# First mixer of a two-layer encoder step: attention chunks read back into the place of their own low parts, and the last value projection in two passes

## The chip, the cores and the metric

The kernel runs on one core of a Trainium2 chip. It is one inference step of a two-layer encoder trunk, all in 32-bit floating point at its inputs and outputs. The metric is the device time of one execution in microseconds (us). Engines: TensorE (PE, with its weight loads PEld), VectorE (DVE), ScalarE (ACT), GpSimd (POOL) and SyncE (SP). SP does no arithmetic here; it issues most of the loads, in order. GpSimd issues the stores and a few loads.

## The reference

1024 prompt rows and 128 sample rows (8 streams of 16), 1152 in all, each 1024 wide, go through two layers. Only the first layer's mixer is touched by the change:

```python
def stick_breaking(q, k, v, q_pos, k_pos):
    z = jnp.einsum('bqhd,bkhd->bhqk', q, k).astype(jnp.float32) * (HEAD_DIM ** -0.5)
    mask = k_pos[None, :] < q_pos[:, None]
    log_keep = jnp.where(mask, jax.nn.log_sigmoid(-z), 0.0)
    between = lax.cumsum(log_keep, axis=3, reverse=True) - log_keep
    w = jnp.where(mask, jnp.exp(jax.nn.log_sigmoid(z) + between), 0.0)
    return jnp.einsum('bhqk,bkhd->bqhd', w.astype(v.dtype), v)

q, k, v, u = ab_project(h, w_in)                # 8 heads of 64, and a gated convolution input u
a_out = stick_breaking(q, k, v, ...)            # 512 columns
c_out = silu(layernorm(depthwise_conv31(u)))    # 512 columns
out = jnp.concatenate([a_out, c_out], axis=-1) @ w_out
```

The layer's input is normalised (RMS) ahead of the projection, the mixer's output is added to the input, and a squared-ReLU MLP follows. The second layer has banded softmax attention in place of the two branches.

## The kernel before, in words

**Data layout.** Activations lie transposed: 128 of the 1024 columns are one *chunk*, with all 1152 rows along the free dimension, cut into three *groups* of 384 (G, NG). Every operand of a dense product is split into a high and a low part (`split`, L183: ScalarE copies the high part, VectorE subtracts it), and each product is three matmuls (`SPLIT`: high·high, high·low, low·high). The eight chunks of a mixer's input, high and low, lie in sixteen fixed tiles, `a{c}{i}` with chunk c and part i (`place`, L231). The eight chunks of the mixer's output, called `cat0`, are put in the same sixteen places later: 0 to 3 are the four pairs of attention heads, 4 to 7 the convolution.

**Steps.** Work is written as lists of `Step`s (L45): a piece of code with its planned TensorE time (`pe`, in ns), a planned VectorE time (`dve`), and, where needed, a name, the name of a step that it comes after, and a lag in planned time behind that step. `merge` (L53) interleaves several lists so that each advances at the same share of its own total; a step whose predecessor or lag isn't due lets the others go first. `level` spreads convolution taps among the result by VectorE time. The framework then writes one instruction queue per engine, in about that order, but takes an instruction ahead when by its own estimates its data and its buffers are ready. On the chip each queue runs in order, and an instruction that waits holds up all behind it.

**Dense products.** `chunk_steps` (L310) makes one output chunk: a step that loads weights ahead, and for each of the three groups two halves of 12 matmuls (`dense`, L215, `per=12`: input chunks 0 to 3, then 4 to 7) into one PSUM bank, and an eviction. There are eight PSUM banks, all of one pool (`bank`, L143).

**First mixer** (`mixer0`, L657). The heads go in four pairs, p = 0 to 3. Stage p does pair p's attention; merged with it are the projection of pair p+1 (`proj`, L872: queries, keys, values, into tiles `sq`, `sk`, `sv`), the cached attention of the sample streams (`sample_steps`, L546), and convolution taps on VectorE. `expand_qk` (L887) makes the attention operands of a pair from `sq` and `sk` (VectorE at L351 and L353). `expand_v` (L906) turns the values: VectorE differences (L903), transposes on TensorE (L913), copies on ScalarE (L915). An attention job has two score steps (L943 to L947, then scans on VectorE, L923 to L929) and a tail (transposes L388, products L398, and the end of a piece in L411 and L412). Each pair's finished pieces go to DRAM (`cat_d`, L363) for p < 3; pair 3's are split directly into chunk 3 of `cat0`.

**Stage 3** has no projection to fill it. In its place it does the first part of the output projection, `part_out` (L1088): input chunks 0 to 2 of `cat0` for all eight output chunks, in passes of 6 and 3 matmuls, added to the input (`xo`, in the places of `sq` and `sv`, loaded by `old`, L1094), and stored. `first` is the weight load and the first passes of 6 of output chunk 0, which need input chunks 0 and 1 only. Beside it runs `conv_norm` (L1020), the layer norm of the convolution output, which reads it from DRAM and writes chunks 4 to 7. The rest of the output projection (chunks 3 to 7) follows in `rest` (L1299).

**What the change touches.** Chunks 0 to 2 come back from DRAM in `ready_chunks` (L1075): for each chunk one load of 1152 columns into the tile `sk` (one buffer, before that pair 3's keys), and three splits from it into the chunk's two places. In stage 3's list of fill work stand, in this order, chunks 0 and 1, `first`, chunk 2 (3000 ns of planned time after the last step carried over from pair 2), and 5000 ns behind it the rest of `part_out`.

Of the kernel before, what the change touches and what calls it, by code (L numbers as in the profile page):

```python
# [9 lines left out]
F32R = mybir.dt.float32r  # L10
# [114 lines left out]
def tile_trunk(ctx, tc, ins, outs):  # L125
# [17 lines left out]
    def bank(name):  # L143
        return psum.tile([P, 512], F32, tag="ps", name=name)
# [109 lines left out]
    def new_hs(name):  # L254
        return [[new_h(g, half, name) for half in range(2)] for g in range(NG)]
# [54 lines left out]
    def chunk_steps(n, got, ahead, h, ks, evac, name, depth=1, per=12):  # L310

        steps = [Step(0.0, lambda: [ahead(n + d) for d in range(depth + 1)], 1200.0)]
        for g in range(NG):
            box = {}

            def ps(g=g, box=box):
                if "p" not in box:
                    box["p"] = bank(f"ps{name}{g}")
                return box["p"]

            steps += dense(ps, lambda: got[n], h, g, ks, per)
            steps.append(Step(0.0, lambda g=g, ps=ps: evac(ps(), g), 470.0))
        return steps

    def chunks_steps(ns, got, ahead, h, ks, evac, name, depth=1):

# [330 lines left out]
    def mixer0():  # L657
        with ExitStack() as st:
# [213 lines left out]
            def proj(p):  # L872
                steps = []
                for n, tag in enumerate(("sq", "sk", "sv")):
                    def evac(ps, g, n=n, tag=tag):
                        if g == 0:
                            S[tag, p] = pp.tile([P, T], F32, tag, f"{tag}0{p}")
                        if g < 2:
                            tt(S[tag, p][:, g * G:g * G + G], ps[:, :G], rstd[g], ALU.mult)
                        else:  # L880
                            ACT(S[tag, p][:, g * G:], ps[:, :G], AF.Copy)
                        if g == 2 and n:
                            put(outs["sb_k" if n == 1 else "sb_v"][p], S[tag, p])
                    steps += chunk_steps(at[4 * n + p], got, ahead, h, ks, evac, f"p{p}{n}")
                return steps

# [98 lines left out]
            for p in range(4):  # L985
                S["p"] = p
                expand_qk(p)
                if p < 3:
                    fill = proj(p + 1)
                    if p < 2:  # L990
                        fill[10:10] = ag(p + 2)
                    n = TAPS[p + 1]
                    mix, now, taps = [], taps[:n], taps[n:]
                else:
                    cat_t = new_hs("cat0")
                    (first, fill), now = part_out(0, range(3), pp, cat_t), []
                    for s in taps:
                        s.pe = 900.0
                    mix = taps + conv_norm(lambda: (conv_pool.close(), Bufs(st.enter_context(pool("ln")), t1=3, yl=5))[1],
                                           cat_t)  # L1000
                cat = Cat(0, p, wk, cat_t)
                jobs = attend(p, cat)
                body, left = pipeline(jobs[1:], jobs[0][2])
                steps = carry + [jobs[0][0]] + [Step(327.0, lambda p=p, g=g: expand_v(p, g)) for g in range(NG)]
                if p == 3:
                    late, = ready_chunks(0, [2], pp, cat_t)
                    late.name, late.after, late.lag = "ready", carry[-1].name, 3000.0
                    fill[0].after, fill[0].lag = "ready", 5000.0
                    fill = ready_chunks(0, range(2), pp, cat_t) + first + [late] + fill
                steps += [jobs[0][1]] + body  # L1010
                carry = left
                if p == 3:
                    steps += carry
                cs = sample_out(cat, wk, p)
                load = sample_caches(0, p, cp)
                sample = two_samples(*(sample_steps(0, p, bg, S, wk, load, soft, cs) for bg in range(2)))
                run(level(merge(steps, sample, fill, mix), now))
            return cat_t

    def conv_norm(new_pool, cat_t):  # L1020

        steps = []

        pools = []

        def norm(g):
            box = {}

            def load():
                if g == 0:  # L1030
                    pools.append(new_pool())
                box["y"] = [pools[0].tile([P, G], F32, "yl", f"yl{g}{c}") for c in range(4)]
                for c in range(4):
                    put(box["y"][c], cat_d[0][4 + c, :, g * G:g * G + G])

            def centre():
                yl = box["y"]
                mu = bank(f"mu{g}")
                for c in range(4):
                    mm(mu[:, :G], ones, yl[c], start=c == 0, stop=c == 3)  # L1040
                for c in range(4):
                    stt(yl[c], mu[:, :G], -1.0 / 512, yl[c], ALU.mult, ALU.add)

            def squares():
                yl, box["acc"] = box["y"], None
                for c in range(4):
                    box["acc"] = add_square(box["acc"], yl[c], pools[0], f"l{g}{c}")

            def scale():
                box["r"] = pools[0].tile([P, G], F32, "r", f"rl{g}")  # L1050
                diag, box["rows"], _ = rstd_of(box["r"], pools[0], box["acc"], 1.0 / 512, LN_EPS, f"l{g}")
                diag(box["acc"])

            def out(c):
                y = box["y"][c]
                tt(y, y, box["r"], ALU.mult)
                s = pools[0].tile([P, G], F32, "t1", f"ls{g}{c}")
                gg, bb = cvec[:, 1, c:c + 1], cvec[:, 2, c:c + 1]
                ACT(s, y, AF.Sigmoid, bias=bb, scale=gg)
                ACT(y, y, AF.Identity, bias=bb, scale=gg)  # L1060
                tt(y, y, s, ALU.mult)
                split(cat_t[g][1][0][:, c, :], cat_t[g][1][1][:, c, :], y)

            name = f"ln{g}"
            return ([Step(50.0, load, 0.0, f"l{name}"),
                     Step(2600.0, centre, 1900.0, f"c{name}", f"l{name}", 4000), Step(500.0, squares, 1400.0),
                     Step(700.0, scale, 1200.0, f"s{name}", f"c{name}", 5000),
                     Step(800.0, lambda: box["rows"](), 0.0, None, f"s{name}", 2500)]
                    + [Step(300.0, lambda c=c: out(c), 1500.0) for c in range(4)])

        for g in range(NG):
            steps += norm(g)
        return steps

    def ready_chunks(layer, chunks, pp, cat_t):  # L1075

        steps = []
        for c in chunks:
# [5 lines left out]
                    split(hi, lo, cr[:, g * G:g * G + G])  # L1084
            steps.append(Step(300.0, go))
        return steps

    def part_out(layer, ks, pp, cat_t):  # L1088

# [900 lines left out]
```

## Time and profile before

Times of three runs: 2721.12, 2721.54 and 2724.41 us; the median is 2721.54.

| | |
|---|---|
| profiled execution | 2724.12 us |
| its span, first to last instruction | 2722.3 us |
| mean granted TensorE clock | 0.993 |
| TensorE / weight loads | 2667.6 / 2555.7 us busy |
| VectorE / ScalarE / GpSimd | 2038.3 / 1362.9 / 330.2 us busy |
| DMA | 422.89 MB, mean 155 GB/s |

A row of a view in stretches gives the stretch and its length, then each engine's busy time in it with the count of instructions, the granted clock as a share of full speed, the busy share of the 16 DMA engines and GB/s. A row of a timeline gives start, duration, engine, line of the kernel, operation, output and inputs by the program's names, shapes and count; in brackets stands the idle time of the engine ahead of it and what ended it. A row of a list of waits gives who waited for whom: us in total, times, longest. A row of the chain of waits gives start, duration and what the time went to. TensorE records overlap (the next starts inside the one before), so the cost of a pass is read from start to start.

### The profile page before, as it was taken

The numbers are of one execution on the slowest core, as the hardware profiler recorded it, in microseconds if no ns is written. First come the engines' busy times: TensorE is split into PE (matmuls) and PEld (weight loads), VectorE is DVE, ScalarE is ACT, GpSimd is POOL, SyncE is SP. The second block draws the span as 40 slices with busy tenths as digits, with TensorE's granted clock in tenths as the row PEclk, the third lists the DMA queues.
The fourth block names the chain that finished last, engine by engine and source line by source line (L and its number), as shares of the span: only waits on it lengthen the run. The fifth ranks groups of instructions, "written<-read, shape, count | busy, mean of one in ns | idle before, by whom it ended". The sixth has DMA issues, their size and how long they took to land.

```text
span 2722.3 us, 50512 instructions
## 1 busy us (share of the span) xinstructions
PE 2667.6 (98%) x19362; PEld 2555.7 (94%) x19362; DVE 2038.3 (75%) x4105; ACT 1362.9 (50%) x2854; POOL 330.2 (12%) x599
## 2 busy tenths in 40 slices
PE   8999998999999999999999999999999999999998
PEld 8888886899999999999999999997999999999998
DVE  7999996887777755768577777778787777647587
ACT  6344456755555533445355555555554555534344
POOL 1000111131111100000011111110321111100001
PEclk9999999999999999999999999999999999999999
DMA  4344447544333486335444444446533334674344
GB/s 159 104 128 150 142 139 247 171 146 143 139 138 138 152 281 231 110 109 183 145 135 134 139 141 138 138 132 217 185 136 140 145 140 147 234 255 136 96 125 146
DMA packets 173202, 422.89 MB, mean 155 GB/s; under 512 B 25968, under 2 KB 53808, under 8 KB 170912
## 3 DMA queue, kind: packets, MB, share of 16 engines
q1 hardware_dynamic: 135696, 288.38, 32.6%
q0 software_dynamic: 37120, 131.27, 14.0%
q8 instruction: 152, 2.49, 0.4%
q14 instruction: 90, 0.74, 0.1%
q10 hardware_dynamic: 144, 0.02, 0.0%
HBM read 289.60 MB, written 117.34 MB: 149 GB/s over the span
## 4 chain that ended last, share of the span: by engine, by line
PE 82%; DVE 9%; DMA 4%; ACT 3%; issue 2%; SPq 0%; POOL 0%; DVEq 0%; ACTq 0%; POOLq 0%
PE pd L1709 25%; PE um L1484 25%; PE psc L225 10%; PE psp L225 4%; PE avc L469 2%; PE psoa L225 2%; PE tpc L457 2%; DMA cr<-cat_d 1%; PE f L225 1%; PE zs L570 1%; DVE y L737 1%; PE zc L1220 1%; PE ava L398 1%; PE so L604 1%; PE psg L225 1%
## 5 line engine op out<-in xcount | busy, mean ns | idle before, releaser
L225 PE MATMUL psc<-h,hl_wc 128*128 128x384 f32 x1728 | 328.4, 339 | 0.0
L225 PEld LDWEIGHTS psc<-h,hl_wc 128*128 128x128 f32 x1728 | 297.0, 188 | 9.2 <-issue 7.9
L1484 PE MATMUL um<-sl,hl_m 128*128 128x288 f32 x1548 | 241.1, 296 | 0.0
L1484 PEld LDWEIGHTS um<-sl,hl_m 128*128 128x128 f32 x1548 | 218.6, 189 | 0.0
L1709 PE MATMUL pd<-tm,hl_wd 128*128 128x288 f32 x1584 | 214.7, 294 | 0.0
L1709 PEld LDWEIGHTS pd<-tm,hl_wd 128*128 128x128 f32 x1584 | 211.3, 189 | 0.0
L737 DVE SCALAR_TENSOR_TENSOR y<-u,dw,y 128x1024 f32<-128x1024 f32 (+1 forms) x232 | 177.6, 807 | 0.7
L1491 ACT ACTIVATE hdm<-hdm 128x288 f32<-128x288 f32 x192 | 84.7, 442 | 156.5 <-DVE hdm L1490 154.7
L225 PE MATMUL psp<-h,hl_wi 128*128 128x384 f32 x864 | 162.4, 340 | 0.0
L186 DVE TENSOR_TENSOR tm<-xr,tm 128x576 fp32r<-128x576 f32 (+1 forms) x120 | 85.7, 715 | 96.5 <-ACT tm L185 96.2
L225 PEld LDWEIGHTS psp<-h,hl_wi 128*128 128x128 f32 x864 | 148.3, 188 | 6.2 <-issue 5.1
L185 ACT ACTIVATE tm<-xr 128x576 fp32r<-128x576 f32 (+1 forms) x120 | 77.5, 646 | 94.1 <-PE pd L1709 74.7
L1484 PE MATMUL um<-sl,hl 128*128 128x288 f32 x756 | 119.1, 296 | 0.0
L1709 PE MATMUL pd<-th,hl_wd 128*128 128x288 f32 x792 | 113.4, 296 | 4.2 <-DVE th L186 4.1
L1709 PEld LDWEIGHTS pd<-th,hl_wd 128*128 128x128 f32 x792 | 107.9, 189 | 5.1 <-DVE th L186 4.5
L1709 PE MATMUL pd<-xr,hl_wd 128*128 128x288 f32 x792 | 112.7, 296 | 0.0
L1709 PEld LDWEIGHTS pd<-xr,hl_wd 128*128 128x128 f32 x792 | 108.3, 190 | 0.0
L1187 ACT ACTIVATE s<-s,mxc 128x640 f32<-128x640 f32 (+4 forms) x128 | 88.8, 694 | 38.0 <-DVE mxc L1184 36.6
L1484 PEld LDWEIGHTS um<-sl,hl 128*128 128x128 f32 x756 | 106.4, 188 | 0.8
L185 ACT ACTIVATE whc<-tpc 128x512 fp32r<-128x512 f32 (+1 forms) x144 | 72.1, 523 | 66.1 <-PE tpc L457 63.8
L1709 PE MATMUL pd<-tm,hl 128*128 128x288 f32 x768 | 104.9, 295 | 0.0
L1184 DVE CUSTOM_DVE_ANT_0 s<-zc,bp 128x384 f32<-128x384 f32 (+3 forms) x128 | 66.2, 518 | 50.0 <-PE zc L1221 48.9
(530 smaller groups left out, 6575.3 us busy)
## 6 DMA issues: line engine op xcount, KB each, us to landing
xr<-hb_d SPq DMA_DIRECT2D x208, 288.0 KB, 2.9
xr<-in_w_up_dram SPq DMA_DIRECT2D x64, 512.0 KB, 4.1
hb_d<-hdm POOLq DMA_DIRECT2D x96, 288.0 KB, 2.4
hb_d<-t POOLq DMA_DIRECT2D x96, 288.0 KB, 2.4
wm<-in_w_down_dram SPq DMA_DIRECT2D x64, 256.0 KB, 3.8
st_wd<-in_w_down_dram SPq DMA_DIRECT2D x64, 256.0 KB, 3.3
st_wc<-in_w_in_c_dram SPq DMA_DIRECT2D x44, 256.0 KB, 3.0
xm_d<-xo POOLq DMA_DIRECT2D x16, 576.0 KB, 3.9
```

The lines of the kernel that those rows point to most:

```text
L185: ACT(hi, src, AF.Copy)
L186: return tt(lo, src, f(hi), ALU.subtract)
L225: mm(ps()[:, :G], hl[:, a, at:at + P], act[g][k // 4][b][:, k % 4, :], start=n == 0, stop=n == len(todo) - 1)
L398: mm(st["av"][64 * m:64 * m + 64, o0:o0 + n], vs[:, j, i], st["w"][gi][:, c0:c0 + n], start=gi == 0, stop=gi == last)
L457: nc.tensor.transpose(tp[:, c0 + q * P:c0 + (q + 1) * P], blocks.get(j, tile_q), ident)
L469: mm(st["av"][:, o0:o0 + n], vs[:, j, i].rearrange("p a d -> p (a d)"), src[:, c0:c0 + n], start=st["done"] == 0, stop=st["done"] == nmm - 1)
L737: stt(src if j == CW - 1 else dst, src, wj, dst, ALU.mult, ALU.add)
L1184: nc.vector.tensor_tensor_reduce(s[:, c:c + m], z, b, -1.0, mx, ALU.add, ALU.min, new)
L1187: ACT(s[:, :n], s[:, :n], AF.Exp, bias=mx, scale=-1.0, accum_out=tot)
L1484: mm(banks[b, n][:, :TQ], w[:, a, c * P:c * P + P], combo(key, c)[:, h, n * TQ:n * TQ + TQ], start=k < 3 and c == 0 and i == 0, stop=c == ...
L1491: ACT(y, y, AF.Relu)
L1709: mm(ps, w[:, a, m * P:m * P + P], b[:, h, (n - ns[0]) * TQ:(n - ns[0]) * TQ + TQ], start=first and s == 0, stop=j == NJ - 1 and s == 2, s ...
```

## The change

Three things. The value projection of pair 3 is cut by `halves_steps`: the first halves of its three groups (input chunks 0 to 3) stay at the end of stage 2's fill, into three banks; the second halves (chunks 4 to 7) and the evictions go to the front of stage 3's fill. `read_back` loads a chunk of `cat0` directly into the place of its own low part, and `split_back` splits it there: the high part is copied out, and the low part is subtracted in place. Chunks 0 and 1 are loaded after the first halves, at the end of stage 2's fill; chunk 2 after the steps carried over from pair 2. The order and the lags of stage 3 are set to suit: both score steps of the first job come ahead of the turning of V, which waits for the last eviction and 3000 ns; the rest of `part_out` comes after V is turned and 2000 ns after chunk 2 is split; the mean of the convolution is due 7000 instead of 4000 ns after its load. `cat0`'s places are named one stage earlier.

```diff
+    def halves_steps(n, got, ahead, h, ks, evac, name):
+        early, late = [Step(0.0, lambda: [ahead(n + d) for d in range(2)], 1200.0)], []
+        for g in range(NG):
...
+            one, two = dense(ps, lambda: got[n], h, g, ks)
+            early.append(one)
+            late += [two, Step(0.0, lambda g=g, ps=ps: evac(ps(), g), 470.0)]
+        return early, late
...
+                    if (p, n) == (3, 2):
+                        early, late = halves_steps(at[11], got, ahead, h, ks, evac, "p32")
+                        late[-1].name = "p32"
+                        S["late"] = late
+                        steps += early + [Step(0.0, lambda: (read_back(0, 0), read_back(0, 1)))]
+                        continue
...
-                steps = carry + [jobs[0][0]] + [Step(327.0, lambda p=p, g=g: expand_v(p, g)) for g in range(NG)]
+                turned = [Step(327.0, lambda p=p, g=g: expand_v(p, g)) for g in range(NG)]
+                steps = carry + [jobs[0][0]] + turned + [jobs[0][1]] + body
                 if p == 3:
-                    late, = ready_chunks(0, [2], pp, cat_t)
-                    late.name, late.after, late.lag = "ready", carry[-1].name, 3000.0
-                    fill[0].after, fill[0].lag = "ready", 5000.0
-                    fill = ready_chunks(0, range(2), pp, cat_t) + first + [late] + fill
-                steps += [jobs[0][1]] + body
+                    turned[0].after, turned[0].lag, turned[-1].name = "p32", 3000.0, "v3"
+                    steps = (carry + [Step(0.0, lambda: read_back(0, 2), 0.0, "back")] + [*jobs[0][:2]] + turned + body)
+                    late = split_back([2], cat_t)
+                    late[0].after, late[0].lag, late[-1].name = "back", 9000.0, "ready"
+                    fill[0].after = "v3"
+                    fill = (S["late"] + split_back(range(2), cat_t) + first + late
+                            + [Step(0.0, int, 0.0, None, "ready", 2000.0)] + fill)
...
-                     Step(2600.0, centre, 1900.0, f"c{name}", f"l{name}", 4000), Step(500.0, squares, 1400.0),
+                     Step(2600.0, centre, 1900.0, f"c{name}", f"l{name}", 7000), Step(500.0, squares, 1400.0),
...
+    def read_back(layer, c):
+        tiles = chunks[f"cat{layer}"]
+        if (c, 1) not in tiles:
+            tiles[c, 1] = place(c, 1, F32R, f"cat{layer}")
+        dma(f(tiles[c, 1]), cat_d[layer][c])
+
+    def split_back(cs, cat_t):
+        def go(c, g):
+            hi, lo = (x[:, c % 4, :] for x in cat_t[g][c // 4])
+            split(hi, lo, f(lo))
+        return [Step(100.0, lambda c=c, g=g: go(c, g), 550.0) for g in range(NG) for c in cs]
```

More of the change, by code (lines that the diff above doesn't have):

```diff
@@ L323, in chunk_steps, with ps @@
         return steps
+    def halves_steps(n, got, ahead, h, ks, evac, name):
+        early, late = [Step(0.0, lambda: [ahead(n + d) for d in range(2)], 1200.0)], []
+        for g in range(NG):
+            box = {}
+            def ps(g=g, box=box):
+                if "p" not in box:
+                    box["p"] = bank(f"ps{name}{g}")
+                return box["p"]
+            one, two = dense(ps, lambda: got[n], h, g, ks)
+            early.append(one)
+            late += [two, Step(0.0, lambda g=g, ps=ps: evac(ps(), g), 470.0)]
+        return early, late
     def chunks_steps(ns, got, ahead, h, ks, evac, name, depth=1):
@@ L988, in mixer0 @@
                 if p < 3:
+                    if p == 2:
+                        cat_t = new_hs("cat0")
                     fill = proj(p + 1)
@@ L994, in mixer0 @@
                 else:
-                    cat_t = new_hs("cat0")
                     (first, fill), now = part_out(0, range(3), pp, cat_t), []
@@ L1000, in mixer0 @@
                                            cat_t)
-                cat = Cat(0, p, wk, cat_t)
+                cat = Cat(0, p, wk, cat_t if p == 3 else None)
                 jobs = attend(p, cat)
                 body, left = pipeline(jobs[1:], jobs[0][2])
-                steps = carry + [jobs[0][0]] + [Step(327.0, lambda p=p, g=g: expand_v(p, g)) for g in range(NG)]
+                turned = [Step(327.0, lambda p=p, g=g: expand_v(p, g)) for g in range(NG)]
+                steps = carry + [jobs[0][0]] + turned + [jobs[0][1]] + body
                 if p == 3:
-                    late, = ready_chunks(0, [2], pp, cat_t)
-                    late.name, late.after, late.lag = "ready", carry[-1].name, 3000.0
-                    fill[0].after, fill[0].lag = "ready", 5000.0
-                    fill = ready_chunks(0, range(2), pp, cat_t) + first + [late] + fill
-                steps += [jobs[0][1]] + body
+                    turned[0].after, turned[0].lag, turned[-1].name = "p32", 3000.0, "v3"
[5 more added lines that the diff above has]
+                            + [Step(0.0, int, 0.0, None, "ready", 2000.0)] + fill)
                 carry = left
```

## The prediction, on record before the change was run

> **What bounds the kernel now.** I began with the page's busy times.
>
> ```profile
> span 2722.3 us, 50512 instructions
> PE 2667.6 (98%) x19362; PEld 2555.7 (94%) x19362; DVE 2038.3 (75%) x4105; ACT 1362.9 (50%) x2854; POOL 330.2 (12%) x599
> ```
>
> TensorE bounds the whole, and only 2% of the span is left to it as idle time. The change touches the first mixer alone, so next I cut that part into stretches of 20 us. Pair 2's stage runs from about 304 to 404 us (its own attention, the projection of pair 3, the last convolution taps), pair 3's from 404 to about 524.
>
> ```profile
> core 0: us, PE busy (x) PEld busy (x) DVE busy (x) ACT busy (x) POOL busy (x), PEclk, DMA share, GB/s
> 304.30:324.30 20.00, 19.88 (x150) 17.38 (x148) 19.70 (x27) 11.23 (x26) 5.64 (x9) 1.00 0.71 200
> 324.30:344.30 20.00, 19.20 (x141) 15.71 (x142) 17.94 (x29) 8.91 (x24) 1.66 (x3) 1.00 0.52 170
> 344.30:364.30 20.00, 20.00 (x171) 15.95 (x170) 17.33 (x27) 10.26 (x23) 1.05 (x2) 1.00 0.56 182
> 364.30:384.30 20.00, 20.00 (x162) 17.50 (x161) 18.52 (x28) 13.04 (x34) 2.69 (x5) 1.00 0.42 129
> 384.30:404.30 20.00, 20.00 (x178) 17.70 (x177) 18.98 (x30) 10.60 (x23) 2.55 (x5) 1.00 0.30 85
> 404.30:424.30 20.00, 11.80 (x64) 6.94 (x63) 8.68 (x15) 8.72 (x22) 5.38 (x10) 0.83 1.04 337
> 424.30:444.30 20.00, 17.49 (x126) 13.75 (x125) 16.30 (x36) 14.09 (x33) 1.11 (x2) 1.00 0.48 144
> 444.30:464.30 20.00, 19.80 (x124) 14.98 (x124) 17.07 (x34) 15.25 (x33) 3.26 (x6) 1.00 0.81 293
> 464.30:484.30 20.00, 20.00 (x188) 16.91 (x186) 14.78 (x33) 14.97 (x34) 0.54 (x1) 1.00 0.52 171
> 484.30:504.30 20.00, 18.41 (x129) 14.17 (x129) 18.34 (x39) 16.75 (x36) 2.70 (x5) 1.00 0.53 181
> 504.30:524.30 20.00, 20.00 (x158) 17.29 (x157) 13.52 (x33) 15.36 (x30) 1.07 (x2) 1.00 0.33 111
> ```
>
> In pair 2's stage TensorE is busy 99.1 of 100 us, and VectorE 92.5. In the first 40 us of pair 3's stage TensorE idles 8.2 + 2.5 = 10.7 us and the granted clock falls to 0.83. The last 80 us idle only 1.8 us. So the room lies in those 40 us. The chain of waits, TensorE's own waits and its timeline say what is waited for there.
>
> ```profile
> 403.35 1.24 DVE l L351
> 404.60 9.62 DMA cr<-cat_d
> 416.32 6.47 DMA cr<-cat_d
> 432.43 6.69 DMA cr<-cat_d
> ```
>
> ```profile
> PE psoa L225 <- ACT cat L185: 8.0, 3, 6.0
> PE tpa L388 <- DVE sg L929: 2.2, 2, 1.3
> PE zs L570 <- ACT qb L561: 1.3, 1, 1.3
> ```
>
> ```profile
> 397.86 2.33 PE L225 MATMUL psp<-h,hl_wi 128*128 128x384 f32 x12
> 400.03 0.39 PE L943 MATMUL z<-k,q 128*128 128x512 f32 x1
> ...
> 419.18 0.64 PE L570 MATMUL zs<-ct03k,qb 128*32 128x256 f32 x8
> 419.75 2.85 PE L1040 MATMUL mu<-yl,ones 128*128 128x384 f32 x8
> 423.39 2.78 PE L225 MATMUL psoa<-cat,hl_wo0a 128*128 128x384 f32 x12 [0.80 <-ACT cat L185]
> ...
> 428.93 0.84 PE L913 MATMUL vt<-ident,sv 128*128 128x128 f32 x6
> ```
>
> The three chunks of the attention output come back one after the other through a single buffer, the old place of pair 3's keys: the first load cannot start before L351 has read those keys, the others not before the chunk ahead is split. TensorE stands in its queue at the output projection for 8.0 us of the 10.7.
>
> **The change, part by part.** Its terms are made against the profiled execution: 2724.12 us, of which 1.8 lie outside the span. That execution is 2.58 us above the median of the three runs, 2721.54; I take the difference off at the end.
>
> (1) *Half of the value projection leaves pair 2's stage.* Three passes of 12 matmuls move. One takes 400.03 - 397.86 = 2.17 us from start to start, three 6.5 us. With them go two VectorE evictions of 0.55 us (the third is ScalarE's):
>
> ```profile
> L879 DVE TENSOR_TENSOR sv<-psp,rh x2: 545/548/552, 387.7 to 395.4; 128x384 f32<-128x384 f32 x2
> ```
>
> If TensorE alone set this stage's length, it would shorten by the 6.5 us and, at most, the 0.9 of idle: 7.4. If VectorE set it and kept its 7.5 us of idle time, only by the 1.1 us of evictions. The truth lies between, since after the change both want almost the same: TensorE 99.1 - 6.5 = 92.6 us, VectorE 92.5 - 1.1 = 91.4. Of VectorE's idle time the greatest part is one kind of wait:
>
> ```profile
> DVE cpa L412 <- ACT ata L411: 6.2, 5, 2.4
> ```
>
> It waits there for ScalarE and so for TensorE's L398, and should wait less once TensorE is ahead. I take the middle of the bounds, **-4.3 us**.
>
> A rule speaks against the -4.3. The Trainium skill (Perfetto Trace Analysis, "Identifying the Most-Contended Engine") holds matmul busy time to be no measure of TensorE's headroom and takes the busy share of weight loads instead. That share is 84 of 100 us here, below VectorE's 92.5, so by the rule VectorE bounds this stage and the term is -1.1. It is the first rival below.
>
> (2) *The three passes go into the front of pair 3's stage*: **+6.5 us** of TensorE work, evictions beside it.
>
> (3) *The read-backs no longer use the key buffer.* A chunk lands in the place of its own low part, which the two-pass order frees once chunks 0 to 3 of the input have been used. Loads 0 and 1 are issued after the last early pass, near the end of pair 2's stage; load 2 after pair 2's last piece. No instruction of the splits is added or removed, nine copies on ScalarE and nine subtractions on VectorE:
>
> ```profile
> L186 DVE TENSOR_TENSOR cat<-cr,cat x9: 551/552/560, 414.8 to 440.6; 128x384 fp32r<-128x384 f32 x9
> ```
>
> Hidden as before, they cost nothing; with that cover gone, nine times 0.55 would be 5 us.
>
> The first load took 9.6 us on a full bus (1.04 of the engines, row above). From the start of pair 3's stage TensorE has, without any chunk of the output: the end of pair 2 (3.3 us of work below), four groups of cached keys (419.75 - 419.18 = 0.57 each, 2.3), the late passes 6.5: 12.1 us, more than the 9.6.
>
> ```profile
> 404.30:409.30 5.00, 3.26 (x24) 1.92 (x22) 4.85 (x9) 3.52 (x11) 1.59 (x3) 1.00 1.05 279
> ```
>
> So 8.0 us of waits go; of the 10.7 I leave the two waits of 1.3 that have nothing to do with it (the sticks' L929, the queries' L561) and one small wait for a split, 0.8 as at 423.39: 3.4 stay. That is **-7.3 us**, with bounds of -10.7 (nothing waits) and 0 (other waits fill the place).
>
> (4) *The clock.* After the long wait the records are slow:
>
> ```profile
> 409.30:414.30 5.00, 0.00 (x0) 0.00 (x0) 0.27 (x1) 0.30 (x2) 3.18 (x6) 0.72 1.03 397
> 414.30:419.30 5.00, 4.49 (x25) 3.05 (x29) 2.63 (x4) 2.47 (x6) 0.62 (x2) 0.60 1.10 331
> 419.30:424.30 5.00, 4.05 (x19) 1.97 (x16) 0.93 (x2) 2.43 (x5) 0.00 (x0) 1.00 0.99 342
> ```
>
> 4.49 us at a clock of 0.60 hold 4.49 x 0.40 = 1.8 us of loss. If no single wait nears 6 us, this goes: **-1.8 us**, bounds -1.8 and 0.
>
> (5) *Pair 3's values are ready later in the plan*, behind the late passes, with the first attention product behind them. Before, the transposes of V ran only at 428.93, 24.6 us after the stage began, because TensorE had been held up ahead of them. Now the late passes end some 14 us in; eviction 0.5, the difference instruction 1.2 and six splits of 0.55 queued ahead on VectorE make about 19. Cover is the first output products (18 x 0.18 = 3.3 us) and the mean of the convolution (2.9). Nothing is added: **0**, bounds -1.3 and +2.6 (one of the waits of 1.3 less, two more).
>
> (6) *Queues.* SP issues every load in order. Read-back 2 waits there for the last put of pair 2, and key loads, weights and residual loads wait behind it. Before, that put went out at 409.87:
>
> ```profile
> 409.87 0.55 POOL L363 DMA_DIRECT2D cat_d<-cpa x1 [0.96 <-DVE cpa L412]
> ```
>
> ```profile
> 387.43 15.31 SPq L539 DMA_DIRECT2D ct03k<-in_sb_k_dram  x3
> ```
>
> Three of the four key tiles of the first half are asked for before it, so I cost it at 0; the residuals move behind V's transposes, out of the crowded first 10 us. The longer planner lags only move the mean step in the order: 0.
>
> Sum: -4.3 + 6.5 - 7.3 - 1.8 = **-6.9 us**, so 2717.2 for a profiled run and 2721.5 - 6.9 = **2714.6** for the median. Best ends together: -7.4 + 6.5 - 10.7 - 1.8 - 1.3 = -14.7 us. Worst: -1.1 + 6.5 + 0 + 0 + 2.6 = +8.0.
>
> **The rivals.** A measurement here tells 0.2%, 5.4 us, from no change.
>
> *VectorE bounds pair 2's stage.* For it: 92.5 busy, the highest after TensorE. Against: TensorE shows no gap at all from 344 to 404. Then term (1) is -1.1 and the sum -3.7: 2717.8, no measurable change.
>
> *The read-backs are hidden no better.* Both are issued within 2 us of each other, just as the keys and the convolution's rows load at 397 GB/s. If the second lands after twice 9.6 = 19.2 us, the 12.1 us of cover plus the mean's 2.9 (L1040) leave 4.2 us of waiting, and I count the clock's fall again (+1.8): -6.9 + 6.0 = -0.9 us, 2720.6.
>
> *Banks: the rival on the slower side.* The three early passes each hold one of eight PSUM banks, from about 83%, 90% and 97% of pair 2's stage (steps 13, 14 and 15 of 15) until the late passes, planned at 2, 7 and 12% of pair 3's: a mean of some 24 us. Scores and transposes go through banks:
>
> ```profile
> L947 ACT ACTIVATE sg<-z 128x512 f32<-128x512 f32 (+3 forms) x30 | 14.0, 507 | 2.3 <-PE z L944 2.1
> L390 ACT ACTIVATE wa<-tpa 128x512 f32<-128x512 f32 (+1 forms) x23 | 12.1, 564 | 5.5 <-PE tpa L388 5.5
> ```
>
> That is 53 turns in 100 us, 13 in 24. If each then makes TensorE wait as its waits for ScalarE and VectorE do now, 2.2 / 2 = 1.1 us, it costs 14.3 us: +7.4, 2728.9. It decides from a wait of (6.9 + 5.4) / 13 = 0.95 us. Against it: three output banks and two score banks are held at 424 to 444 already, with 2.5 us of idle in 20.
>
> *Everything fits*: near the best ends, about -12: 2709.5.
>
> The change may also not do what it says, if the queues' written order puts the early and late passes together again; that is 2721.5.
>
> **How the numbers follow.** Forecast 0.50; everything fits 0.12; VectorE 0.13; read-backs 0.08; no effect 0.04; banks 0.13. Around the forecast the middles of (1) and (3) are uncertain by about 3 us, so of its 0.50 some 0.38 lie beyond -5.4. Faster 0.38 + 0.12 + 0.02 (of VectorE) = 0.52; slower 0.13; within 0.2% 0.35. The range is 2709 to 2725: it leaves out most of the banks and the very best ends, 0.17 together.
>
> **What would show it.** Right: TensorE's wait at the output projection for the split of a chunk falls from 8.0 us to under 2 in all; the granted clock stays 1.00 through 404 to 424; the read-backs are issued before pair 2's last transposes end and land within 10 us; pair 3's stage starts 3 to 6 us earlier, and VectorE is busier than 95% before it. Wrong: gaps in front of scores and transposes from 385 to 415 released by ScalarE (banks); a wait over 3 us for a read-back; first products of pair 3 later than 430; or a stage of pair 2 as long as before.

## The result: a little slower, and the profile after

The changed kernel takes 2726.66 us (median of 20 runs, 2721.40 to 2730.96), the kernel before 2721.13 beside it (20 runs). The ratio is 1.0017, with a 95% interval of 1.0011 to 1.0024, so the change costs 4.6 us (3.0 to 6.5). The ratio is taken over all these runs; the two medians stand 5.5 us apart. The forecast was 6.9 us less, and its range ended at 2725. The profiled execution after took 2725.53 us. The head of its page:

```profile
span 2723.7 us, 50504 instructions
PE 2666.5 (98%) x19362; PEld 2554.9 (94%) x19362; DVE 2038.5 (75%) x4105; ACT 1362.1 (50%) x2854; POOL 331.4 (12%) x599
```

The work is the same; only its order and its waits can differ. Executions reach the first mixer some us apart, so I compare lengths of stages between three marks of TensorE's timeline that every kernel here has: the last of pair 2's earlier sample products (`so<-ct01v`), the turning of pair 2's last samples (`sq`), with which its stage ends, and the first matmul of the next part of the output projection (`psob`). Before:

```profile
316.64 1.08 PE L604 MATMUL so<-ct01v,sw 128*32 128x128 f32 x32
...
404.60 0.27 PE L612 MATMUL sq<-ident,sb 128*128 128x128 f32 x1
...
520.29 4.95 PE L225 MATMUL psob<-cat,hl_wo0b 128*128 128x384 f32 x27
```

and after:

```profile
310.01 1.08 PE L621 MATMUL so<-ct01v,sw 128*32 128x128 f32 x32
...
395.76 0.27 PE L629 MATMUL sq<-ident,sb 128*128 128x128 f32 x1
...
519.42 5.83 PE L225 MATMUL psob<-cat,hl_wo0b 128*128 128x384 f32 x32
```

From the first mark to the second, pair 2's stage went from 88.0 to 85.8 us, 2.2 shorter. From the second to the third, pair 3's stage went from 115.7 to 123.7 us, 8.0 longer, where forecast terms (2) to (4) make it 2.6 shorter (+6.5 - 7.3 - 1.8). Together the two are 5.8 longer. The stretches of 20 us of the profile after, from the end of pair 2's stage on, show the idle time in its old amount:

```profile
395.50:415.50 20.00, 15.52 (x95) 10.59 (x94) 9.81 (x18) 8.11 (x17) 5.79 (x10) 0.88 0.92 285
415.50:435.50 20.00, 15.45 (x97) 11.54 (x96) 14.01 (x25) 12.47 (x33) 1.09 (x2) 0.78 0.43 137
435.50:455.50 20.00, 18.37 (x117) 14.28 (x118) 15.10 (x34) 16.14 (x35) 2.73 (x5) 1.00 0.71 224
```

In the 60 us after the end of pair 2, TensorE idles 4.5 + 4.6 + 1.6 = 10.7 us; before it was 8.2 + 2.5 + 0.2 = 10.9. But 6.5 us more work stands there now, and the clock is down in two of the stretches, not in one. Estimated as busy time times what is missing of full speed, that costs 15.52 x 0.12 + 15.45 x 0.22 = 5.3 us, against 11.80 x 0.17 = 2.0 before. TensorE's waits of the first mixer, after, have other names:

```profile
PE vt L936 <- ACT sv L927: 4.6, 1, 4.6
PE mu L1067 <- DMA yl<-cat_d: 4.5, 2, 2.5
PE tpa L405 <- DVE sg L952: 2.4, 2, 1.5
...
PE z L966 <- DVE cpa L429: 1.0, 1, 1.0
```

The 8.0 us at the output projection for a chunk's split are gone, as meant. In their place stand 4.5 us for the rows of the convolution's mean and 4.6 us for the values of pair 3. TensorE's timeline after shows the two:

```profile
405.53 1.86 PE L225 MATMUL psp<-h,hl_wi 128*128 128x384 f32 x9
409.42 0.88 PE L1067 MATMUL mu<-yl,ones 128*128 128x384 f32 x2 [2.03 <-DMA yl<-cat_d]
412.75 4.21 PE L1067 MATMUL mu<-yl,ones 128*128 128x384 f32 x6 [2.46 <-DMA yl<-cat_d]
...
418.97 0.79 PE L225 MATMUL psp<-h,hl_wi 128*128 128x384 f32 x3
...
427.01 2.18 PE L936 MATMUL vt<-ident,sv 128*128 128x128 f32 x9 [4.55 <-ACT sv L927]
```

The mean (`mu`) stands in the queue inside the last of the three late passes, after 9 of its 12 matmuls. While TensorE waits for the mean's rows, the last 3 matmuls of the value projection wait too: they run at 418.97, 11.6 us after the ninth. All that makes pair 3's values ready comes behind them, as the timeline of the other engines, after, shows:

```profile
401.22 0.57 POOL L757 DMA_DIRECT2D cat_d<-u  x1 [0.78 <-DVE u L754]
...
409.17 2.13 POOL L1061 DMA_DIRECT2D yl<-cat_d  x4 [5.92 <-DMA cat_d<-u]
...
419.83 0.49 ACT L898 ACTIVATE sv<-psp 128x384 f32<-128x384 f32 x1
...
420.61 0.55 POOL L900 DMA_DIRECT2D out_sb_v_dram<-sv  x1 [9.32 <-ACT sv L898]
...
424.25 1.35 DVE L951 TENSOR_TENSOR_SCAN kps<-kps 128x576 f32<-128x576 f32 x1
425.52 1.20 DVE L926 TENSOR_TENSOR sv<-sv 128x1023 f32<-128x1023 f32 x1
```

The mean reads the convolution output from DRAM. Its last channels are stored from 401.22 on, when the last taps of VectorE are done, and GpSimd waits 5.92 us for that store to land before it issues the loads. The values are evicted at 419.83 and stored to the output at 420.61; only when that store has read them can the differences (L926) overwrite them in place. It landed 4.0 us after its issue, at 424.6. VectorE shows no idle time for it here: the differences run straight behind a scan (`kps`) that stands ahead of them in its queue.

Before, both were there as well, as GpSimd's timeline and the row of the values' store among the transfers show:

```profile
403.35 0.55 POOL L740 DMA_DIRECT2D cat_d<-u  x1 [0.55 <-DVE u L737]
...
405.58 0.54 POOL L883 DMA_DIRECT2D out_sb_v_dram<-sv  x1 [0.78 <-ACT sv L881]
...
412.78 1.60 POOL L1034 DMA_DIRECT2D yl<-cat_d  x3 [1.26 <-DMA cat_d<-u]
```

```profile
yl<-cat_d POOLq DMA_DIRECT2D x5, 192.0 KB, 6.2
out_sb_v_dram<-sv POOLq DMA_DIRECT2D x1, 576.0 KB, 9.0
```

The values' store landed at 405.58 + 9.0 = 414.6, the mean's loads of 412.78 some 6.2 us later. Neither showed as a wait of TensorE: it stood for the read-backs, and asked for the mean at 419.75 and for the values at 428.93. One thing has also moved. Counted from the first mark, the last channels' store goes out at 403.35 - 316.64 = 86.7 us before, 1.3 ahead of the end of pair 2's stage; after it is 401.22 - 310.01 = 91.2, 5.5 behind that end. TensorE leaves the stage sooner, VectorE's taps end later.

So the theory to test is: **the read-back waits were a cover**. Under them lay other late data, and a wait removed only hands TensorE on to the next. Rivals: the mean's place in the order is at fault, and with the mean later the forecast comes true; the two passes themselves cost more than they free (term 1 is wrong); or the crowded DMA engines set all of these waits, whatever the order.

### The profile page after: what moved, and what is told of

Its sections match the earlier page's. It is cut to its first block, busy times and chain, and to the rows that moved or that the text cites. A ratio compares the mean times of both kernels' runs of the same rounds, so it can differ in the third digit from the quotient of the medians.

```text
span 2723.7 us, 50504 instructions
## 1 busy us (share of the span) xinstructions
PE 2666.5 (98%) x19362; PEld 2554.9 (94%) x19362; DVE 2038.5 (75%) x4105; ACT 1362.1 (50%) x2854; POOL 331.4 (12%) x599
## 4 chain that ended last, share of the span: by engine, by line
PE 70%; DVE 6%; ACT 1%; DMA 1%; issue 1%; DVEq 0%; ACTq 0%; SPq 0%
PE pd L1751 26%; PE um L1526 25%; PE psc L225 10%; PE avc L486 2%; PE tpc L474 2%; PE zc L1262 1%; PE zc L1263 1%; PE psoa L225 1%; PE zs L587 1%; PE so L621 1%; DVE xr L1432 0%; DVE s L1231 0%; DMA cr<-cat_d 0%; DVE sl L1756 0%; ACT t L1838 0%
```

## The experiments

Stages measured between the same three marks, in us against the kernel before; the time is the ratio of the runs against the kernel before on the same chip, in us of its median.

| kernel | pair 2's stage | pair 3's stage | ratio (95%) | us |
|---|---|---|---|---|
| the change | -2.2 | +8.0 | 1.0017 (1.0011 to 1.0024) | +4.6 |
| mean_16us | -3.8 | +3.2 | 1.0002 (0.9992 to 1.0011) | +0.5 |
| mean_12us | -3.8 | +4.5 | 1.0000 (0.9991 to 1.0009) | 0.0 |
| reads_only | 0.0 | -3.3 | 0.9983 (0.9974 to 0.9992) | -4.6 |
| halves_only | -3.8 | +8.8 | 1.0020 (1.0009 to 1.0031) | +5.4 |
| v_aside | -3.8 | +3.7 | 0.9994 (0.9986 to 1.0003) | -1.6 |
| v_aside_mean16 | -3.8 | +4.4 | 0.9993 (0.9985 to 1.0002) | -1.9 |
| reads_mean12 | 0.0 | -1.2 | 0.9997 (0.9988 to 1.0006) | -0.8 |
| reads_mean16 | 0.0 | +0.1 | 0.9998 (0.9989 to 1.0007) | -0.5 |
| reads_xolate | 0.0 | -2.9 | 0.9989 (0.9980 to 0.9997) | -3.0 |
| reads_light | 0.0 | -1.1 | 0.9993 (0.9984 to 1.0002) | -1.9 |
| reads_again | 0.0 | -2.4 | 0.9984 (0.9975 to 0.9993) | -4.4 |

The sum of the two stages and the timed difference agree within 2.5 us in every row, so what is looked for does lie in these two stages.

### The mean of the convolution later: mean_16us, mean_12us

The changed kernel with one number changed, the planner's lag of the first mean behind its load:

```diff
-  Step(2600.0, centre, 1900.0, f"c{name}", f"l{name}", 7000)
+  Step(2600.0, centre, 1900.0, f"c{name}", f"l{name}", 7000 if g else 16000)    # 12000 in mean_12us
```

> The changed kernel with one number altered: the first mean of the convolution is due 16000 instead of 7000 ns of planned time after its load, which puts its matmuls behind the transposes of V in TensorE's queue. Theory M (in the changed kernel TensorE stands at this mean, whose rows aren't loaded yet, and the last value pass and with it V are queued behind it): the waits of 4.5 us at the mean and 4.6 us at V's transposes go, with about 2 us of the clock; 2726.7 - 9 to 11 = 2716 to 2718 us. Theory P (the three moved passes are themselves what costs, and the waits only show slack): 2725 to 2728. Theory B (banks held by the early passes make scores and transposes wait): 2725 to 2728.

> The same with 12000 ns: the mean then stands behind the last value pass but still just ahead of V's transposes. Theory M: the last pass is free, TensorE reaches the mean some 5 us later and waits 0 to 3 us there, V's wait falls to under 2; 2719 to 2722 us, between the changed kernel and the one with 16000 ns. Theories P and B: 2725 to 2728.

With 16000 the mean's wait is gone and the time falls to that of before, 1.0002. But one wait has grown. Of TensorE's waits:

```profile
PE vt L936 <- ACT sv L927: 6.1, 1, 6.1
```

and from the timeline of the other engines in that kernel, with VectorE's own reason:

```profile
403.99 0.57 POOL L757 DMA_DIRECT2D cat_d<-u  x1 [0.77 <-DVE u L754]
...
410.71 0.49 ACT L898 ACTIVATE sv<-psp 128x384 f32<-128x384 f32 x1 [1.00 <-PE psp L225]
411.74 2.13 POOL L1061 DMA_DIRECT2D yl<-cat_d  x4 [5.72 <-DMA cat_d<-u]
...
413.87 0.55 POOL L900 DMA_DIRECT2D out_sb_v_dram<-sv  x1
...
421.08 1.23 DVE L926 TENSOR_TENSOR sv<-sv 128x1023 f32<-128x1023 f32 x1 [6.34 <-DMA out_sb_v_dram<-sv]
```

The values are evicted 12 us sooner, counted from the end of pair 2's stage: at 410.71, 12.2 us behind it, where it was 24.1. Their store then stands on GpSimd's queue behind the mean's loads, which wait 5.72 us for the convolution's store. It goes out at 413.87, and the differences wait for it until 421.08. So even with the mean out of the way, the values hang on a transfer that nothing in the arithmetic needs. With 12000 both waits remain, smaller (3.8 for the values, 1.1 for the mean, 2.4 for the layer norm's `rr_l`), and the time is the same. Both expectations took the wait for the values to fall with the mean's, which it did not; the time with 16000, 2722.45 us, missed its 2716 to 2718, and that with 12000, 2721.65, lies in its range. Moving the mean takes back 4 to 5 us of the loss and brings no gain: as the only cause it falls.

### Each part alone: reads_only, halves_only

reads_only leaves the value projection whole at the end of pair 2's stage and keeps the read-backs into the low parts' places; halves_only keeps the two passes and takes the chunks through the keys' old buffer again. Both keep the new order and lags of stage 3 (both score steps ahead of the turning of V, the mean due at 7000, the rest of `part_out` behind V). No run has that order alone, so each part's share below includes it.

```diff
 # reads_only
-  early, late = halves_steps(at[11], got, ahead, h, ks, evac, "p32")
-  late[-1].name = "p32"
-  S["late"] = late
-  steps += early + [Step(0.0, lambda: (read_back(0, 0), read_back(0, 1)))]
+  steps += chunk_steps(at[11], got, ahead, h, ks, evac, "p32")
+  steps += [Step(0.0, lambda: (read_back(0, 0), read_back(0, 1)))]
+  S["late"] = []
...
-  turned[0].after, turned[0].lag, turned[-1].name = "p32", 3000.0, "v3"
+  turned[-1].name = "v3"
 # halves_only
-  steps += early + [Step(0.0, lambda: (read_back(0, 0), read_back(0, 1)))]
+  steps += early
...
-  late = split_back([2], cat_t)
+  late = ready_chunks(0, [2], pp, cat_t)
...
-  fill = (S["late"] + split_back(range(2), cat_t) + first + late
+  fill = (S["late"] + ready_chunks(0, range(2), pp, cat_t) + first + late
```

> Only the reading back into the place of the low parts; the value projection of pair 3 stays whole in pair 2's stage as before the change, and no pass moves. Theory M: pair 2's stage is as long as before the change, the waits of 8.0 us for read-backs go, but TensorE comes to the mean some 4 to 6 us sooner than before the change and waits there for its rows; 2717 to 2720 us. Theory P: without the moved passes the read-backs bring their full gain, 2711 to 2714. If the read-backs cost by themselves (loads on a full bus, splits in place): 2722 or more.

> Only the value projection in two passes; the three chunks come back one after the other through the key buffer as before the change. Theory M: the mean stands ahead of the last value pass as in the changed kernel, the same waits show, and the read-backs are hidden behind them or add up to 3 us; 2725 to 2729 us. Theory P: the same or a little less than the changed kernel, 2725 to 2727. If instead the read-backs are what costs: 2715 to 2719.

The two parts have opposite signs, and both times lie in the range of theory M. The read-backs alone are 4.6 us faster, the two passes alone 5.4 us slower. TensorE's waits with the read-backs alone:

```profile
PE rr_l L285 <- DVE sq_l L281: 4.1, 1, 4.1
PE mu L1066 <- DMA yl<-cat_d: 3.0, 2, 2.0
```

8.0 us of read-back waits went, and 7.1 us came in two others: the mean's rows, and the row of reciprocal roots (`rr_l`) that the layer norm works out after the mean. The gain is what is left, and a clock that fell less. Its stretches from the end of pair 2's stage:

```profile
397.80:417.80 20.00, 15.76 (x110) 9.65 (x113) 12.30 (x23) 10.85 (x29) 5.41 (x10) 1.00 1.01 307
417.80:437.80 20.00, 15.62 (x105) 11.23 (x98) 17.30 (x37) 16.79 (x38) 1.47 (x3) 0.91 0.54 178
437.80:457.80 20.00, 20.00 (x149) 15.97 (x147) 13.75 (x27) 9.97 (x24) 2.88 (x6) 1.00 0.73 234
```

Idle 4.2 + 4.4 + 0 = 8.6 us against 10.9 before. The loss by the clock, estimated as above, is 1.4 us here and 2.0 before. Together -2.9, and the stage is 3.3 shorter.

In halves_only TensorE waits for neither keys nor chunks but for the same two as after the whole change:

```profile
PE mu L1067 <- DMA yl<-cat_d: 6.1, 2, 3.6
PE vt L936 <- ACT sv L927: 5.0, 1, 5.0
```

Here the chunks still come through one buffer, and yet no wait for a chunk is left: the late passes and these two waits cover it. That is why the read-backs, worth 4.6 us alone, bring only 0.8 us on top of the two passes (1.0017 against 1.0020, less than the intervals can tell).

### The values free of their store: v_aside, v_aside_mean16

The differences of pair 3 go to a tile of their own (the place of its keys, which the read-backs no longer need), so they need not wait for the store to have read the values. The second kernel also has the mean's lag of 16000.

```diff
-  tt(v[:, 1:TP][:, ::-1], v[:, 0:TP - 1][:, ::-1], v[:, 1:TP][:, ::-1], ALU.subtract)
-  ACT(v[:, 0:1], v[:, 0:1], AF.Copy, scale=-1.0)
+  d = S["dv"] = pp.tile([P, T], F32, "sk", "dv3") if p == 3 else v
+  tt(d[:, 1:TP][:, ::-1], v[:, 0:TP - 1][:, ::-1], v[:, 1:TP][:, ::-1], ALU.subtract)
+  ACT(d[:, 0:1], v[:, 0:1], AF.Copy, scale=-1.0)
...
-  nc.tensor.transpose(tp[:, i * P:(i + 1) * P], v[:, c:c + P], ident)
+  nc.tensor.transpose(tp[:, i * P:(i + 1) * P], (S["dv"] if c < TP else v)[:, c:c + P], ident)
```

> The changed kernel with the mean due at 16000 ns and, besides, pair 3's value differences written into another tile (the free place of pair 3's keys) instead of over the values. Theory S (with the mean out of the way, what holds V up is the store of V to its output: the differences overwrite V and wait 6.3 us for the store to land): the wait of 6.1 us at V's transposes falls under 1.5 and the time by 4 to 5 us against the kernel with the mean at 16000 alone, to about 2718 where the kernel before stands at 2722. Theory P (the moved passes themselves cost, 6.5 us into the front against 3.9 out of pair 2's stage): the same time as with the mean at 16000 alone, 2722.

> The changed kernel with only the differences written aside; the mean stays where the change has it, ahead of the last value pass. Theory S with theory M: V's eviction is still late behind the mean, and VectorE is busy with other scans until just before the differences; 1 to 3 us less than the changed kernel, 2724 to 2726. If the store alone were the cause: 2720 to 2722.

v_aside is 6.3 us faster than the change (0.9994 against 1.0017), and its wait for the values is 1.1 us where it was 4.6. The profiles show 4.3 us of it in pair 3's stage and another 1.6 in pair 2's, where of these profiles only that of the change has a fall of the clock (last section). The expectation was 1 to 3 us; the measured time, 2721.18, lies in the range written for the store as the only cause. VectorE's row shows what moved:

```profile
423.13 1.20 DVE L927 TENSOR_TENSOR dv<-sv 128x1023 f32<-128x1023 f32 x1
```

The late passes end as late as after the change (their last three matmuls start at 419.81, 23.9 us into the stage), and the last eviction starts at 420.67. But the differences now stand ahead of the scan of `kps` and start 2.5 us behind that eviction, where it was 5.7. So the dependence on the store did its harm through the order of VectorE's queue, and not through a wait that the profile of the change shows. The other waits:

```profile
PE mu L1068 <- DMA yl<-cat_d: 4.9, 2, 3.0
PE psoa L225 <- ACT cat L185: 2.2, 1, 2.2
```

The mean is still waited for, 4.9 us. Moved later as well, it is waited for no more; but then come the keys' scores and the layer norm's own sums, and the time stays the same (0.9993):

```profile
PE zs L587 <- ACT sg L971: 3.8, 1, 3.8
PE ms_l L263 <- DVE sq_l L296: 2.1, 1, 2.1
```

Its expectation added up the two gains (2718); they don't add (2721.72). With either wait taken away another takes its place, which is the theory's claim in its plainest form.

### The read-backs with the mean later: reads_mean12, reads_mean16

reads_only with the mean's lag at 12000 and 16000, by the same line as above.

> The read-backs alone (value projection whole, in pair 2's stage) with the first mean due at 12000 ns, behind V's transposes. Theory M: the 3.0 us at the mean go, and most of the 4.1 us at the layer norm's rows behind it, since other work comes between; 2713 to 2715, 3 to 4 us less than the read-backs alone. If the mean is only where TensorE would stand anyway for want of work: 2717.

> The same with 16000 ns. Theory M: the same gain, 2712 to 2715, unless the layer norm now ends too late for the stage's end, which would show as waits at the end of pair 3's stage; then 2715 to 2718.

Both miss their expectations. The mean's wait goes, and the gain goes with it: 0.9997 and 0.9998. TensorE's waits with 16000:

```profile
PE zs L587 <- DMA ct03k<-in_sb_k_dram: 5.5, 1, 5.5
PE rr_l L285 <- DVE sq_l L281: 2.4, 1, 2.4
```

The next in the queue is the fourth tile of cached keys. Its load can go out only when the first tile's products have freed a buffer (SP waits 9.0 us for `zs` there, five times), and the loads of these tiles landed 8.5 us after their issue there (median of 6). In reads_only that tile was asked for 7 us after the mean, at 417.58, with no wait. So the mean's lag of 7000 is good for the read-backs, and by the results of mean_16us bad for the two passes: the same number serves one part and not the other.

### Are the DMA engines the limit? reads_xolate, reads_light, reads_again

In the profiles with the parts alone and before, the 16 DMA engines are 0.97 to 1.04 busy over the first 20 us of pair 3's stage (1.01 in the row of reads_only above). reads_xolate is reads_only with the load of the residual input behind the late chunk's read-back; reads_light leaves out, besides, the store of pair 3's values, so that output is missing.

```diff
-  dma(f(tiles[c, 1]), cat_d[layer][c])
+  prior["back"] = dma(f(tiles[c, 1]), cat_d[layer][c])
...
+  with tc.issue_after(prior["back"].ins):
       dma(xo[fc].rearrange("p (g t) -> p g t", g=NG), ins["x"][:, :, fc, :].rearrange("g p t -> p g t"))
 # reads_light
-  if g == 2 and n:
+  if g == 2 and n and (p, n) != (3, 2):
```

> The read-backs alone, and the twelve-part load of the residual input, which was issued at 399.85 us ahead of the late chunk's read-back, is held on SP's queue until that read-back has been issued; the order of TensorE's work is unchanged. In the run with the read-backs alone TensorE still stood 3.0 us for the mean's rows of the convolution, over two waits, with the DMA engines busy for all of 394 to 414 us. Theory that the crowded DMA engines make those rows late: with 0.58 MB less ahead of them the wait falls to about 1.5 us and the time by 1 to 2 us against the read-backs alone, to about 0.9977 of the kernel before. Rival, that the rows are late by their own chain (the last taps, their store, their load) whatever else moves: the wait stays at 2.5 to 3.5 us and the ratio at 0.9983. A third way, that the input comes late at the first normalisation and takes the place of the wait: VectorE's conversion of the residual input is named in the waits, and the ratio is 0.999 to 1.001.

> As the run before this one, and the store of pair 3's value projection to the output is left out (that output is missing, 1.15 MB less in the crowded stretch, and nothing waits for it). Theory that the crowded DMA engines set the mean's rows and the fourth key tile: the wait for the mean's rows falls below 0.7 us, and the time to about 0.9970 of the kernel before (3 us less than with the read-backs alone, less what other stores gain). Rival, that the rows are late by their own chain: wait 2 to 3 us, ratio 0.998. Since less is moved here, a gain says how much the full DMA engines cost and not that a kernel could have it.

> The read-backs alone once more, beside the two runs above on one chip. If its gain is one of the schedule, the ratio is 0.9983 again within 0.0010 and TensorE's waits at the head of pair 3 are those seen before (rows of the rotary layer norm about 4, mean's rows about 3 us). If it was a chance of one chip, the ratio lies at 0.9995 to 1.0005.

The repeat gives 0.9984, so the gain of the read-backs alone is no chance of one chip. In reads_xolate the mean's wait is 1.9 us, against 3.0 in reads_only but 2.2 in the repeat on the same chip, and the time did not fall (0.9989). TensorE's waits there:

```profile
PE rr_l L285 <- DVE sq_l L281: 4.1, 1, 4.1
...
PE mu L1066 <- DMA yl<-cat_d: 1.9, 3, 0.9
```

With still less to move, reads_light waits 1.9 us for the mean too, and is no faster (0.9993). Both miss the theory of the crowded engines: it is worth 0.3 to 1.1 us of one wait, and no gain of time shows. A doubt remains: the order of TensorE's work is not quite the same in these two (in both a few matmuls changed places some 35 us into pair 3's stage, against what the first expectation says; in reads_light a wait of 1.4 us for a residual sum is new), so 0.9989 and 0.9993 are not pure prices of the bytes. The `rr_l` wait, 4.1 us in all three kernels as in reads_only, hangs on the layer norm's own chain behind the mean. In reads_mean12 it is gone, and waits for cached keys (4.0) and for split chunks (1.9) stand in its place.

## Why the prediction was wrong

The runs split the 4.6 us into three steps, by three comparisons one after the other: the read-backs alone -4.6; from there to v_aside, which is the two passes with the values free of their store, +3.0; from there to the change +6.3. They add up by construction. By the intervals each is uncertain by 2.5 to 3.4 us, so the +3.0 is not clear of the noise; the two stages of the profiles give -3.3, +3.2 and +5.9 for the same steps. The forecast had -9.1 (terms 3 and 4), +2.2 (1 and 2) and 0 (5): more than half of the miss is in the last. In another order the shares differ: behind the two passes the read-backs bring only 0.8.

**Step (1), half of the projection leaves pair 2's stage: right in its size, and yet not a gain.** Forecast -4.3, the middle between two bounds, so that it came out this near is in part luck. The stage is 3.8 us shorter in each of the five other kernels with two passes, and 2.2 in the profiled execution of the change, which lost 1.6 to its clock. In halves_only, from the last of the sample products to the end of the stage:

```profile
314.30:397.60 83.30, 79.94 (x662) 66.31 (x653) 77.52 (x114) 47.08 (x113) 8.60 (x16) 1.00 0.53 164
```

TensorE is busy for 79.9 of 83.3 us and VectorE for 77.5 (93%, where I expected over 95%). TensorE's waits there are 3.4 us, all for VectorE, where it was 0.9 before. So both bound the stage in turn. What I didn't follow is VectorE's own end: the convolution's last store goes out 89.6 to 89.7 us after the first mark in those five kernels, against 86.7 before. So TensorE's 3.8 us were won against work of VectorE that then ends in pair 3's stage, where the mean needs it. The rule of the Trainium skill that stood against the term (Perfetto Trace Analysis, "Identifying the Most-Contended Engine": judge TensorE's headroom by its weight loads, or by its share of peak arithmetic, and take the engine with the highest occupancy) made it -1.1. As a forecast of the stage's length the traces don't bear it out; its warning, that VectorE was the engine with least room, they do.

**Step (2), the passes in front of pair 3: right.** +6.5 of work; from reads_only to v_aside pair 3's stage grows by 7.0.

**Steps (3) and (4), read-backs and clock: the read-backs right in mechanism and too large, the clock wrong in its condition.** Forecast -7.3 and -1.8 together -9.1; alone they brought -4.6 and -4.4. In reads_only no chunk was waited for, and the 8.0 us of waiting at the output projection went to nothing. But I left only the three small waits standing that the profile of before already showed. The mean's rows (3.0) and the reciprocal roots (4.1) showed no wait there, because TensorE came to them later. The bound "0 (other waits fill the place)" was the right thought without a name, and the name could have been read: the mean's loads went out at 412.78 and took 6.2 us, for matmuls at 419.75, a slack of about 0.8 us, and 6.0 of the 8.0 us of waiting that I took out stand ahead of them. I even counted this mean as 2.9 us of cover. The clock's loss was to go if no single wait nears 6 us. After the change the longest is 4.6 us, and the loss is 5.3 us instead of 2.0 by the estimate above; with the read-backs alone (longest 4.1) it is 1.4. Several shorter gaps did what I had put down to one long one.

**Step (5), the values of pair 3 later: the step that failed.** I put it at 0, with +2.6 as the worst; freeing the values of their store gave 6.3 us back in the timed runs, 4.3 in pair 3's stage of the profiles. I listed what computes the values (eviction, difference, splits), but not the store that reads them before the in-place difference may write; it took 9.0 us before, under the cover. In mean_16us VectorE stood 6.3 us for it; in the change the differences stood behind other work in VectorE's queue, until v_aside freed them. And I took the end of the late passes as 14 us into the stage. On the chip it was 24 (395.76 to 419.76), since the mean was placed inside the third pass and held back its last three matmuls. With the mean later (mean_16us) the values are evicted 12 us into the stage, and the store alone still keeps the differences to 421.08, 22.5 us into it.

**Step (6), queues: wrong in one place.** "The longer planner lags only move the mean step in the order: 0". The lag decided what stood behind TensorE's wait: the two settings above 7000 took 4 to 5 us off the change. No run has the change with the old 4000, so what the step from 4000 to 7000 itself did stays open.

**The rivals.** Banks, the one on the slower side, has the time (2728.9 against 2726.66) and not the mechanism: it needed 14 us of waits of scores and transposes. After the change the list above has 1.0 us for a score and 2.4 for transposes, both for VectorE, and from 385 to 415 us TensorE waits for nothing but the mean's rows. "Read-backs hidden no better" falls with the waits for chunks, which are gone. "VectorE bounds pair 2's stage" falls as a price of that stage, but its mechanism is in the result: VectorE's late taps are what the mean waits for. That the change does not do what it says is refuted by the stage's length. Of the marks that I named for a wrong forecast, one appeared: pair 3's first products with its values ran at 439.39, later than 430 (before 437.43, in a stage that began 8.8 us later, so the kernel before shows that mark too). Of the marks for a right one, the waits for chunks went and the first two read-backs were issued at 394.19, ahead of the stage's end, but the clock did not stay at 1.00 (0.88).

**The version to keep** is the read-backs alone: 0.9983 and 0.9984 on two chips, about 4.5 us faster than the kernel before and 9 faster than the change as made. The two passes add some 3 us even with the values freed of their store, as terms (1) and (2) of the forecast had it (+2.2): they pay only if they cover more than that, and the read-backs landed in time without them.

## What to carry to other kernels

A long wait of the bounding engine is a cover: before counting it as a gain, walk the engine's queue behind it and write down for each instruction when its data was really ready, stores ahead of in-place writes and read-backs through DRAM included; the gain ends at the first of these. A piece of work that is moved takes with it everything that hangs on its result, transfers too, and a planner's lag that was harmless under the cover can then decide the order. Try each part of a compound change alone: here one part alone gained 4.6 us and the other lost 5.4.

## What the runs showed of the hardware

**The clock fell after a single gap of 1.5 us, in one of six profiled executions that have it.** In the profiled execution of the change TensorE stood 1.47 us for VectorE in pair 2's stage. Its timeline row, and stretches about it:

```profile
383.15 1.47 PE L405 MATMUL tpa<-ident,sg 128*128 128x128 f32 x6 [1.47 <-DVE sg L952]
```

```profile
381.00:383.15 2.15, 0.68 (x6) 0.47 (x5) 2.15 (x4) 1.18 (x4) 0.00 (x0) 1.00 1.03 330
383.15:385.00 1.85, 1.84 (x8) 1.75 (x9) 1.79 (x4) 0.94 (x2) 0.54 (x1) 0.52 0.31 66
385.00:387.00 2.00, 2.00 (x10) 1.90 (x9) 2.00 (x5) 1.07 (x3) 0.00 (x0) 0.59 0.39 124
387.00:389.00 2.00, 2.00 (x29) 1.75 (x31) 2.00 (x4) 0.00 (x0) 0.00 (x0) 1.00 0.03 7
```

For about 4 us the clock is near half, which costs 1.85 x 0.48 + 2.00 x 0.41 = 1.7 us. In mean_16us, as in the four other kernels with two passes, the same six transposes after the same gap ran at full speed:

```profile
387.53 0.85 PE L405 MATMUL tpa<-ident,sg 128*128 128x128 f32 x6 [1.47 <-DVE sg L952]
```

The Trainium skill (TensorE: Matmul & The Clock Gate, "Part 1: The HAM clock gate (the "warmup" mystery)") has the clock fall to half after an idle window of about 3.4 us, in a window that runs freely, and rise again some 4 us into sustained work. Half speed and about 4 us to come back agree with the trace; the length of the gap does not. Two gaps of 2.0 and 2.5 us with 0.9 us of work between them did the same at the mean (0.50 from 412.75 to 416). Two of 2.0 and 0.9 us in reads_only did not. So short gaps in a row are not free either, and which of them costs differs from one profiled execution to the next.
